# A two-layer transformer block with expert rows: token tiles in turn, and x with a token on each partition from layer 0's rows on

## The chip, the cores and the metric

The kernel runs on one core of a Trainium2 chip. The core has five engines that follow their own instruction streams in order: TensorE (PE in the profile, its weight loads PEld), VectorE (DVE), ScalarE (ACT), GpSimd (POOL) and SyncE (SP). Data come from memory through the core's 16 DMA engines, asked for by queues that belong to SP, ACT and POOL. The metric is the device time of one execution in microseconds.

## The reference

256 tokens of width 1024 pass two layers. Layer 0 mixes tokens by window attention and a gated MLP, layer 1 by means over windows. Each layer then has an expert stage ("PEER"): every token scores 128 + 128 sub-keys for each of 8 heads, takes the best 16 pairs, and gathers 16 rows of `down` and `up` for each head. Cut to what matters here:

```python
def multiscale_pool(h, w_pool, scale):        # layer 1's mixer
    ...                                       # cs: running sums of h, in 4 groups of 256 columns
    for g, w in enumerate((2, 4, 8, 16)):
        lo, hi = jnp.clip(t - w // 2, 0, L_), jnp.clip(t + w // 2, 0, L_)
        mean = (cs[:, hi, g] - cs[:, lo, g]) / (hi - lo)
        diffs.append(mean - hf[:, :, g])
    pooled = jnp.stack(diffs, axis=2)
    return jnp.einsum('blgc,gce->blge', pooled, w_pool).reshape(B_, L_, D_MODEL) * scale

def peer_ffn(h, w_q, sub_keys, down, up):
    q = (xb @ w_q).reshape(n, 8, 2, 128)
    s = jnp.einsum('thpk,pnk->thpn', q, sub_keys)
    s_top, i_top = lax.top_k(s, 16)
    ...                                       # 256 sums of pairs, best 16 again -> idx, gate (softmax)
    act = jax.nn.gelu(jnp.einsum('thkd,td->thk', down[idx], xb))
    return jnp.einsum('thk,thkd->td', gate * act, up[idx])

for l in range(2):
    m = jax.nn.silu(c) @ mod_w[l] + mod_b[l]  # -> sh1, sc1, g1, sh2, sc2, g2
    h = rms_norm(x, norm1_g[l]) * (1 + sc1) + sh1
    y = attn_gmlp_mixer(h, ...) if l == 0 else multiscale_pool(h, pool_w, pool_scale)
    x = x + g1 * y
    h2 = rms_norm(x, norm2_g[l]) * (1 + sc2) + sh2
    x = x + g2 * peer_ffn(h2, ...)
return rms_norm(x, final_g)
```

All arithmetic that decides the choice of rows is held at single precision: a product of two matrices is made from three, with each operand split into a high and a low part (`sH`, `sL` for weights, `xH`, `xL` for x).

## The kernel before

**Layers and stages.** `attention_gmlp` computes layer 0's mixer. Then `peer_rows(0)`, `pool_mixer`, `peer_rows(1)` and `final` follow. From `peer_rows` on, the instructions of each engine run in the order in which the code issues them. x is held as `xT`, a channel on each partition, in 8 blocks of 128 channels by 256 tokens.

**The projection in `peer_rows`.** `norm_split` (L299 to L308) makes xH and xL, `pair_mm` (L340 to L343) the first head's queries, `tile_mm` (L317 to L319) those of the other heads, two tiles a head. The weights come through `Stream`: SP loads an item of 512 KB (three buffers), ScalarE casts half of it to `sH` (L105), VectorE subtracts to `sL` (L108). `scores` (L1040, L1043) follows one tile behind. `advance` puts four steps of `choose` on VectorE behind each tile from head 1 on. `choose` is the selection for one unit (a token tile and a head) in some 22 steps: MAX8, FIND_INDEX8 and MATCH_REPLACE8 (L954 to L962), comparisons (L992 to L997), the row numbers `eid` (L998), and ScalarE's Exp for the gate (L1001). `rows_of` (L950, L951) turns h2 to a token on each partition. Units go head by head, both token tiles of a head in turn.

**The rows.** A ring of 12 slots of 1 MB holds what comes from memory for 128 tokens at a time: one row number k of a unit, `down` and `up` side by side. `fetch` asks for the next row (L1018, on POOL) as soon as the next slot of the ring is free. During the projection xH, xL and hq take three slots. When it is over, the loop over 256 rows (16 units of 16) begins: a dot of `down` with h2 on VectorE (L1102), with two steps of `choose` behind each; behind every fourth row a Gelu on ScalarE (L1108); one row later `weigh` makes the four weights (L1089) and `add_up` makes for each row a diagonal on ScalarE (`dgr`, L1076), two matmuls of `up` into PSUM (L1079) and gives the slot back. In layer 0, VectorE also computes 56 products of modulation weights in this loop, one at every fourth row (L884).

**Between the layers.** When all rows have been asked for, `after_rows` takes ring slots for pool weights and prepares them, a step for every row added up. `residual` copies the four sums out of PSUM (L908, L909), turns them back (L914) and adds them to xT (L916); sums of squares go over partitions by matmul (L175). `pool_mixer` multiplies by pool_w first (L1226), then takes the means (L1254). Layer 1 ends in `residual` and `final`, which turns x back by a matmul with the final gains (L1270) and writes four pieces (L1290).

## Time and profile before

| | |
|---|---|
| median of 3 runs | 1755.05 us (1752.7 to 1755.4) |
| the profiled execution | 1751.43 us |
| its span, first to last instruction | 1749.4 us |
| busy: PE, DVE, POOL, ACT | 1352.9, 1197.8, 741.6, 466.0 us |
| moved by DMA | 622.52 MB, mean 356 GB/s |
| mean granted TensorE clock | 0.896 of full |

Engines are busy for part of the span only, and the DMA share, in tenths for 40 slices of the span, is 9 (90% or more) in all but a few slices. In a timeline, a row is an instruction or a run of equal ones: start, duration, engine, line, operation, what it writes and reads, and in brackets how long the engine was idle before it and what ended that.

### The profile page before, as it was taken

Reading aid. Unit: us, or ns where it says so; the run is one execution under the profiler, and the core shown is the slowest. Engines: PE = TensorE matmul, PEld = TensorE weight load, DVE = VectorE, ACT = ScalarE, POOL = GpSimd, SP = SyncE. Lnnn points to the kernel's source line nnn. Section 1 sums busy time; section 2 is a strip of 40 time slices with the busy share of each in tenths; the row PEclk is TensorE's granted clock in tenths of the full one; section 3 lists DMA queues with packets and bytes.
Section 4 is the critical chain, followed back from the end, with each engine's and each line's share of the span. In section 5 each row is a group of like instructions: output and inputs, shape, how many; then the busy total and the mean of one; then the engine's idle time right before and its main releaser. Section 6 shows DMA issues by size and latency. Waiting matters only on the chain. (4 is left out here: it accounts for less than half of the span.)

```text
span 1749.4 us, 15727 instructions
## 1 busy us (share of the span) xinstructions
PE 1352.9 (77%) x4148; PEld 691.8 (40%) x4148; DVE 1197.8 (68%) x2910; ACT 466.0 (27%) x1176; POOL 741.6 (42%) x632
## 2 busy tenths in 40 slices
PE   7988897677767677767777797877877887777776
PEld 3865793233223233223233387333333333333333
DVE  6987768877787776555554377877777775545443
ACT  3555553222222121111111353222222222111112
POOL 3535433443444434444444133544444454544442
PEclk8987998988888978988888899899998898999899
DMA  7434578999999999999999328799999999999993
GB/s 291 164 109 158 170 280 323 419 419 419 418 419 418 419 418 418 419 419 419 419 419 414 135 86 342 321 419 420 419 419 420 419 420 420 420 420 420 418 420 124
DMA packets 97867, 622.52 MB, mean 356 GB/s; under 512 B 11250, under 2 KB 11762, under 8 KB 31860
## 3 DMA queue, kind: packets, MB, share of 16 engines
q0 software_dynamic: 73728, 536.90, 74.3%
q1 hardware_dynamic: 23328, 83.82, 12.9%
q8 instruction: 34, 0.56, 0.1%
q10 hardware_dynamic: 724, 0.80, 0.1%
q14 instruction: 53, 0.43, 0.1%
HBM read 620.44 MB, written 1.05 MB: 355 GB/s over the span
## 5 line engine op out<-in xcount | busy, mean ns | idle before, releaser
L1079 PE MATMUL ps_big<-row,dgr 128*128 128x512 f32 x2048 | 1033.4, 664 | 340.3 <-ACT dgr L1076 340.3
L1018 POOL DMA_INDIRECT row<-in_DU,eid x512 | 609.6, 1191 | 801.7 <-PE ps_big L1079 537.1
L1102 DVE SCALAR_TENSOR_TENSOR row<-row,h 128x1024 f32<-128x1024 f32 x512 | 627.2, 1225 | 419.4 <-DMA row<-in_DU,eid 407.8
L1079 PEld LDWEIGHTS ps_big<-row,dgr 128*128 128x128 f32 x2048 | 424.2, 212 | 948.1 <-issue 504.8
L1076 ACT ACTIVATE dgr<-cf,cr 128x128 f32<-128x128 f32 x512 | 164.0, 390 | 276.9 <-DVE cr L1089 275.2
L1108 ACT ACTIVATE actr<-actr 128x4 f32<-128x4 f32 x128 | 26.3, 205 | 701.0 <-DVE row L1102 700.8
L108 DVE TENSOR_TENSOR sL<-raw,sH 128x512 fp32r<-128x512 f32 x75 | 57.8, 798 | 30.7 <-ACT sH L105 24.9
L884 DVE SCALAR_TENSOR_TENSOR md<-md,crowb 128x1024 f32<-128x1024 f32 x56 | 68.1, 1216 | 0.0
L317 PE MATMUL ps_a<-row,sH 128*128 128x256 f32 x224 | 65.3, 291 | 2.3 <-ACT sH L105 1.4
L318 PE MATMUL ps_a<-row,sH 128*128 128x256 f32 x224 | 63.1, 282 | 1.0 <-issue 1.0
L319 PE MATMUL ps_a<-row,sL 128*128 128x256 f32 x224 | 63.5, 283 | 0.5 <-DVE sL L108 0.4
L105 ACT CAST sH<-raw 128x512 fp32r<-128x512 f32 x84 | 49.2, 619 | 24.5 <-DMA raw<-in_w_q 10.9
L511 PE MATMUL ps_big<-sH,hH 128*128 128x256 f32 x128 | 38.4, 306 | 8.6 <-ACT sH L105 6.1
L317 PEld LDWEIGHTS ps_a<-row,sH 128*128 128x128 f32 x224 | 42.8, 191 | 4.1 <-ACT qTp L1051 2.1
L319 PEld LDWEIGHTS ps_a<-row,sL 128*128 128x128 f32 x224 | 42.7, 191 | 1.7 <-DVE sL L108 1.1
L318 PEld LDWEIGHTS ps_a<-row,sH 128*128 128x128 f32 x224 | 42.8, 191 | 0.7 <-issue 0.7
L1102 DVE DVE_READ_ACCUMULATOR row<-row,h 128x1 f32 x512 | 42.2, 82 | 0.0
L512 PE MATMUL ps_big<-sL,hH 128*128 128x256 f32 x128 | 38.2, 301 | 2.6 <-DVE sL L108 2.5
L1001 ACT ACTIVATE gater<-best,z 128x16 f32<-128x16 f32 x32 | 9.8, 308 | 106.8 <-DVE z L1000 106.7
L513 PE MATMUL ps_big<-sH,hL 128*128 128x256 f32 x128 | 37.2, 296 | 0.1
L1001 ACT ACT_TABLE_LOAD x28 | 35.9, 1283 | 0.5
L1108 ACT ACT_TABLE_LOAD x28 | 35.9, 1283 | 0.4
(265 smaller groups left out, 1315.6 us busy)
## 6 DMA issues: line engine op xcount, KB each, us to landing
md<-in_modT SPq DMA_DIRECT2D x56, 512.0 KB, 7.9
raw<-in_w_q SPq DMA_DIRECT2D x32, 512.0 KB, 3.3
raw<-in_modT SPq DMA_DIRECT2D x19, 512.0 KB, 4.7
row<-in_DU,eid POOLq DMA_INDIRECT x512, 18.5
pro<-in_modT SPq DMA_DIRECT2D x11, 512.0 KB, 3.7
pro<-in_modA SPq DMA_DIRECT2D x8, 512.0 KB, 6.7
raw<-in_in_w SPq DMA_DIRECT2D x8, 512.0 KB, 4.4
pro<-in_in_w SPq DMA_DIRECT2D x6, 512.0 KB
```

What stands on the lines that cost most here:

```text
L105: k.nc.scalar.copy(hi, src)
L108: eng.tensor_sub(lo, src, hi)
L317: nc.tensor.matmul(ps, lhsT=hi[:, i], rhs=xh[:, kb], start=(first and i == 0), stop=False)
L318: nc.tensor.matmul(ps, lhsT=hi[:, i], rhs=xl[:, kb], start=False, stop=False)
L319: nc.tensor.matmul(ps, lhsT=lo[:, i], rhs=xh[:, kb], start=False, stop=(last and i == 3))
L884: self.nc.vector.scalar_tensor_tensor(raw, raw, 1.0, crow, op0=OP.mult, op1=OP.mult, accum_out=self.m[:, l, j:j + 1])
L1001: nc.scalar.activation(g, best, AF.Exp, bias=z[:, 0:1], scale=1.0, accum_out=z[:, 1:2])
L1018: nc.gpsimd.indirect_dma_start(r, None, a[f"DU{l}"], bass.IndirectOffsetOnAxis(ap=eid[:, tt, h, k:k + 1], axis=0))
L1076: nc.scalar.activation(dg, self.ident, AF.Copy, scale=cw[:, tt, s:s + 1])
L1079: nc.tensor.matmul(acc[2 * tt + hf], lhsT=dg, rhs=r[:, D + 512 * hf:D + 512 * hf + 512], start=(s == 0), stop=(s == P - 1))
L1102: nc.vector.scalar_tensor_tensor(r[:, :D], r[:, :D], 1.0, h2[:, tt], op0=OP.mult, op1=OP.mult, accum_out=act[:, tt, s:s + 1])
L1108: nc.scalar.activation(act[:, tt, s], act[:, tt, s], AF.Gelu_apprx_tanh)
```

## The change

What is done otherwise, in the order of the program:

- `norm_in` now makes xH, xL and h2 for layer 0. x itself is turned to a token on each partition (`self.x`) beside the first rows, and stays so.
- Units go token tile by token tile: eight heads of tile 0, then eight of tile 1. In layer 0, `scores` of head 0 follow `pair_mm` at once and up to 30 steps of `choose` behind them; in layer 1 head 0 is projected for tile 0 alone, scored and chosen, before tile 1.
- The ring has 10 slots instead of 12. Modulation products use the weights' three buffers, at every row with k % 3 == 2.
- Small steps go beside the rows (`beside`, one a row): turning x, spreading a vector of 1024 over partitions (`rowvec`: eight transposes, two copies), and, when token tile 0's rows are added up, its `tile_end`: x plus gate times sum, square with sum, inverse root.
- `after_rows` runs two steps for every row added up. It loads pool_w and the means' matrix, spreads five vectors, and makes tile 0's h1.
- `pool_mixer` takes the means first and multiplies by pool_w then; each token tile gets product, sum, inverse, scaling and shift on VectorE, then transposes to xH and xL.
- The last unit's batches are 4, 4, 4, 2, 1, 1. `residual` and `final` are gone: tile 1's `tile_end` scales and writes two pieces, tile 0's were written in the middle of layer 1.

```diff
-RING = 12
+RING = 10
...
-        units = [(tt, h) for h in range(8) for tt in range(2)]
+        units = [(tt, h) for tt in range(2) for h in range(8)]
...
+        prev = []
+        if l == 0:
+            first = self.pair_mm(xH, xL)
+        else:
+            halves = [st.next() for _ in range(4)]
+            first = [self.bank("a") for _ in range(2)]
+            qT = tk.tile([P, 2, T], F32, name="qTp", bufs=2)
+            for tt in range(2):
+                ts = slice(tt * P, (tt + 1) * P)
+                for p in range(2):
+                    for hf in range(2):
+                        hi, lo = halves[2 * p + hf]
+                        self.half_mm(first[p][:, ts], 4 * hf, hf == 0, hf == 1, hi, lo, xH[:, :, ts], xL[:, :, ts])
+                    nc.scalar.copy(qT[:, p, ts], first[p][:, ts])
+                scores(0, qT, (tt,))
+                if tt == 0:
+                    advance(30)
+            st.ahead(LOOK)
...
+            if h == 0:
+                scores(h, qT)
+                advance(30)
...
+            ends = (4, 8, 12, 14, 15, 16) if n == len(units) - 1 else (4, 8, 12, 16)
...
+    def add_rows(self, tt, src, row, ss):
...
+        for hf in range(2):
...
+            nc.vector.tensor_mul(t, src[hf], row[:, hs])
+            yield
+            nc.vector.tensor_add(self.x[:, tt, hs], self.x[:, tt, hs], t)
...
+            nc.scalar.activation(sq, self.x[:, tt, hs], AF.Square, scale=1.0 / 32, accum_out=ss[:, hf:hf + 1])
+            yield
...
+        for k, col in enumerate(vecs):
+            if k % 2 == 0:
+                t = yield from self.carve(2, D)
+            self.rows_.append(t[:, k % 2])
+            yield from self.rowvec(t[:, k % 2], col)
+        self.h1 = yield from self.carve(2, D)
+        yield from self.scaled(0, self.y[0], *self.rows_[:2], self.h1)
...
+        for tt in range(2):
...
+            run(self.add_rows(tt, z[tt], gs, ss))
+            y = self.inverse(ss, True)
+            run(self.scaled(tt, y, G2, sh2, h2))
+            for hf in range(2):
...
+                for i in range(4):
...
+                    nc.tensor.transpose(pt[:, i * P:(i + 1) * P], h2[:, tt, kb * P:(kb + 1) * P], self.ident)
...
+                nc.scalar.copy(xH[o], p3)
+                nc.vector.tensor_sub(xL[o], p3, xH[o])
```

What this does to the engines' streams, at three places. First ScalarE in layer 0, behind `pair_mm`: casts of weights (`sH`), copies of queries (`qTp`), of scores (`sc`) and of h2, and the Exp of a unit (`gater`). Before:

```order
L1051 COPY qTp<-ps_a 128x256 [waits PE_49] x2
L105 CAST sH<-raw 128x512
L105 CAST sH<-raw 128x512 [waits DMAHW6_49,Activation_49]
L1051 COPY qTp<-ps_a 128x256 [waits PE_49]
L1043 COPY sc<-ps_w 128x512 [waits PE_49]
L951 COPY h_2002<-ps_a 128x512 [waits PE_49]
L105 CAST sH<-raw 128x512 [waits DVE_49]
```

and now:

```order
L1115 COPY qTp<-ps_a 128x256 [waits PE_49] x2
L1090 COPY sc<-ps_w 128x256 [waits PE_49] x2
L1046 ACT_TABLE_LOAD
L1046 ACTIVATE gater,z<-best,z 128x16 [waits DVE_49]
L105 CAST sH<-raw 128x512
L105 CAST sH<-raw 128x512 [waits DMAHW7_49,Pool_49]
L1115 COPY qTp<-ps_a 128x256 [waits PE_49]
L923 COPY h_2004<-ps_a 128x512 [waits PE_49]
```

The scores' copies and the first unit's Exp have moved ahead of the casts for head 1 and of its first copy; the Exp stood some 20 rows further down.

Second ScalarE near the end of layer 0's rows: the diagonals (`dgr`) of a batch of four rows and what stands between them. Before:

```order
L1076 ACTIVATE dgr<-cf,cr 128x128 [waits DVE_49,PE_49]
L1076 ACTIVATE dgr<-cf,cr 128x128 [waits PE_49,Activation_49] x3
L1108 ACTIVATE actr<-actr 128x4 [waits DVE_49]
L1076 ACTIVATE dgr<-cf,cr 128x128 [waits DVE_49,PE_49]
L1076 ACTIVATE dgr<-cf,cr 128x128 [waits PE_49,Activation_49] x2
L1188 CAST ones_r<-ones 128x128
L1213 ACTIVATE row<-row,g_5463 128x256 [waits DMASW6_49,DMASW2_49,DMAHW6_49,DVE_49,PE_49]
L1213 ACTIVATE row<-row,g_5463 128x256
L1076 ACTIVATE dgr<-cf,cr 128x128 [waits Activation_49]
```

and now, where a `row` is a ring slot that takes the spread vectors:

```order
L1142 ACTIVATE dgr<-cf,cr 128x128 [waits DVE_49,PE_49]
L938 COPY row<-ps_a 128x512 [waits DMASW2_49,DMASW4_49,DMASW0_49,DMASW6_49,PE_49,Pool_49]
L938 COPY row<-ps_a 128x512 [waits PE_49]
L1142 ACTIVATE dgr<-cf,cr 128x128 [waits Activation_49]
L938 COPY row<-ps_a 128x512 [waits PE_49] x2
L1142 ACTIVATE dgr<-cf,cr 128x128 [waits Activation_49]
L938 COPY row<-ps_a 128x512 [waits DMASW5_49,DMASW3_49,DMASW7_49,DMASW1_49,PE_49]
L938 COPY row<-ps_a 128x512 [waits PE_49]
L1142 ACTIVATE dgr<-cf,cr 128x128 [waits Activation_49]
L938 COPY row<-ps_a 128x512 [waits PE_49] x2
```

Behind each diagonal there now stand two copies of a spread vector's halves, which wait for TensorE's transposes.

Third VectorE in layer 0, where token tile 0's last rows are weighed: `row,actr` is a dot, `cr` the weights of a batch, `eq` to `gater` steps of `choose`. Before, at the same count of dots:

```order
L1102 SCALAR_TENSOR_TENSOR row,actr<-row,h_2002 128x1024 [waits DMASW0_49,PE_49]
L1089 TENSOR_TENSOR cr<-actr,gater 128x4 [waits Activation_49]
L962 MAX_INDEX ix<-v,wkt 128x8 [waits DVE_49]
L954 MAX v<-sc 128x8
L1102 SCALAR_TENSOR_TENSOR row,actr<-row,h_2002 128x1024 [waits DMASW1_49,PE_49]
L956 MAX_INDEX ix<-v,sc 128x8 [waits DVE_49]
L958 MATCH_REPLACE wkt<-v,sc 128x128
```

and now:

```order
L1177 SCALAR_TENSOR_TENSOR row,actr<-row,h_2004 128x1024 [waits DMASW0_49,PE_49]
L1158 TENSOR_TENSOR cr<-actr,gater 128x4 [waits Activation_49]
L1040 TENSOR_TENSOR eq<-eq,ixf 128x512 [waits DVE_49]
L1042 TENSOR_REDUCE e_4438<-eq 128x32 [waits DVE_49]
L1043 SCALAR_TENSOR_TENSOR eid<-e_4438 128x16 [waits DVE_49]
L1045 TENSOR_SCALAR z<-best 128x1
L951 TENSOR_TENSOR tx<-ps_big,rg 128x512 [waits PE_49]
L1177 SCALAR_TENSOR_TENSOR row,actr<-row,h_2004 128x1024 [waits DMASW1_49]
L1048 RECIPROCAL z<-z 128x1 [waits Activation_49]
```

The product of the sum in PSUM (`ps_big`) with the spread gate now stands between the weights and the next dot.

## Rows read from the trace of the kernel before

**Rows 1.** The page: busy DMA and GB/s in 40 equal slices; the queue of gathers.
```profile
DMA  7434578999999999999999328799999999999993
GB/s 291 164 109 158 170 280 323 419 419 419 418 419 418 419 418 418 419 419 419 419 419 414 135 86 342 321 419 420 419 419 420 419 420 420 420 420 420 418 420 124
q0 software_dynamic: 73728, 536.90, 74.3%
```
**Rows 2.** Timeline, steady rows of layer 1: start, duration in us, engine, line.
```profile
1695.80 1.22 DVE L1102 SCALAR_TENSOR_TENSOR row<-row,h 128x1024 f32<-128x1024 f32 x1 [1.26 <-DMA row<-in_DU,eid]
1697.66 7.13 PE L1079 MATMUL ps_big<-row,dgr 128*128 128x512 f32 x16 [2.55 <-ACT dgr L1076]
1698.30 1.22 DVE L1102 SCALAR_TENSOR_TENSOR row<-row,h 128x1024 f32<-128x1024 f32 x1 [1.19 <-DMA row<-in_DU,eid]
```
**Rows 3.** Windows of 10 us: PE, PEld, DVE, ACT, POOL, PEclk, DMA share, GB/s.
```profile
280.00:290.00 10.00, 8.69 (x15) 3.88 (x16) 9.20 (x31) 3.38 (x11) 2.74 (x3) 0.69 0.27 88
980.00:990.00 10.00, 7.84 (x15) 3.13 (x14) 4.80 (x11) 3.42 (x8) 1.35 (x1) 0.84 0.03 11
1090.00:1100.00 10.00, 1.63 (x2) 0.83 (x3) 8.93 (x26) 3.17 (x8) 0.70 (x1) 0.59 0.51 199
```
**Rows 4.** Timeline, start of layer 0's rows.
```profile
223.23 0.37 ACT L1051 COPY qTp<-ps_a 128x256 f32<-128x256 f32 x1 [1.05 <-PE ps_a L319]
236.78 1.17 POOL L1018 DMA_INDIRECT row<-in_DU,eid  x1 [14.27 <-DVE z L1000]
269.69 1.21 DVE L1102 SCALAR_TENSOR_TENSOR row<-row,h 128x1024 f32<-128x1024 f32 x1
285.37 1.20 POOL L1018 DMA_INDIRECT row<-in_DU,eid  x1 [13.66 <-PE ps_big L1079]
```
**Rows 5.** Timeline of VectorE, the first unit's choice in layer 0.
```profile
220.68 0.30 DVE L954 MAX8 v<-sc 128x8 f32<-128x128 f32 x1 [1.55 <-ACT sc L1043]
229.31 1.29 DVE L108 TENSOR_TENSOR sL<-raw,sH 128x512 fp32r<-128x512 f32 x2 [1.59 <-ACT sH L105]
236.31 0.18 DVE L998 SCALAR_TENSOR_TENSOR eid<-e 128x16 uint32<-128x16 f32 x1
```
**Rows 6.** Gathers from issue to landing: window 1130 to 1400, then the whole run.
```profile
DMA to landing us min/median/max: 15.0/17.8/19.2
DMA to landing us min/median/max: 7.7/18.5/22.7
```
**Rows 7.** Groups by shape: busy us, mean ns of one, idle before, its releaser.
```profile
L951 ACT COPY h<-ps_a 128x512 f32<-128x512 f32 x8 | 4.7, 591 | 0.3
L909 DVE COPY row<-ps_big 128x512 f32<-128x512 f32 x4 | 2.8, 689 | 11.8 <-PE ps_big L1079 11.8
L1226 PE MATMUL ps_big<-row,xT 128*128 128x256 f32 x32 | 7.5, 382 | 0.0
```
**Rows 8.** The chain that ended last: start, us, four transposes in a row.
```profile
1035.25 0.44 PE ps_a L950 x4
```
**Rows 9.** Timeline, from layer 0's last rows to layer 1's first dot.
```profile
976.66 0.16 DVE L1089 TENSOR_TENSOR cr<-actr,gater 128x4 f32<-128x4 f32 x1
985.28 1.23 DVE L1102 SCALAR_TENSOR_TENSOR row<-row,h 128x1024 f32<-128x1024 f32 x1 [1.26 <-DMA row<-in_DU,eid]
989.19 8.83 PE L1079 MATMUL ps_big<-row,dgr 128*128 128x512 f32 x16 [2.16 <-ACT dgr L1076]
1031.27 0.39 PE L317 MATMUL ps_a<-row,sH 128*128 128x256 f32 x1 [0.34 <-ACT qTp L1051]
1052.56 1.04 POOL L1018 DMA_INDIRECT row<-in_DU,eid  x1 [14.85 <-PE ps_a L319]
1086.74 1.21 DVE L1102 SCALAR_TENSOR_TENSOR row<-row,h 128x1024 f32<-128x1024 f32 x1
```
**Rows 10.** Timeline, the tail: the last dot and the last write.
```profile
1723.22 1.23 DVE L1102 SCALAR_TENSOR_TENSOR row<-row,h 128x1024 f32<-128x1024 f32 x1 [1.26 <-DMA row<-in_DU,eid]
1745.02 0.35 ACTq L1290 DMA_DIRECT2D out<-row  x1
```

## What the change will do to the time: the prediction

> **What bounds the kernel now.** I read the page's slices first: from about 290 us to 975 and again from 1110 to 1715 the transfers run at 418 to 420 GB/s, and the queue of gathers alone carries 537 MB [rows 1]. In those stretches a row of experts (1 MB for 128 tokens) lands every 2.49 us, which the distance of two dots shows, and VectorE waits about 1.2 us for each [rows 2]. So a stretch of rows can only be shortened by starting its stream earlier or by moving fewer bytes. The bytes stay the same. What is left are the places where the stream stands still, read from windows and timelines: the start of layer 0's rows (share 0.27 from 280 to 290), the passage between the layers (0.03 in 980 to 990, 0.51 in 1090 to 1100 [rows 3]) and the tail.
>
> How a stream starts: the first gathers go out during the projection, but only into free slots of the ring. Dots begin when the projection is over. The first slot of the loop comes back 15.7 us after the first dot (269.69 to the gather at 285.37 [rows 4]), and until then nothing can be asked for. Hence the start of the steady stream is set by the first dot plus about 21 us, and by how many rows were in before it: 12 now. It is not set by the first gather.
>
> **The change part by part.** I sum against the profiled execution, 1751.4 us; its span is 1749.4, and the median of the runs shown is 3.6 above it.
>
> *Layer 0, first unit at once.* Token tile 0's head 0 is now chosen in one piece. In the trace that choice takes 15.8 us from the first MAX8 to the written indices, with four pairs of splits between (1.3 us a pair) and a wait of 1.6 [rows 5]: 9 us alone. It starts near 217.9, 2.8 before the first MAX8 of now, since three splits instead of five and no tile of TensorE stand ahead of it, so the first gather is ready near 227 instead of 236.8. But ScalarE has the unit's Exp ahead of the next casts and of the copy of head 1's first half out of its bank. With both banks taken, TensorE's next half starts near 229.1, and its copy, which stands at 223.23 now [rows 4], comes at 232.1: 8.9 us late. The rest up to the first dot took 46.5 us (223.23 to 269.69). I keep that; if waiting for weights behind gathers absorbed some, it would be less by up to 5. First dot 278.6, **+8.9** (4 to 11).
>
> *Ring of 10.* Ten rows are in before the loop's first release, where 12 were. Two rows at 2.49 are fetched later, **+5.0** in each layer. That is the same arithmetic in layer 1, where xH and xL leave eight slots and then two.
>
> *Ring of 10 in the steady stretch.* With 12 slots a row lands 15.0 to 19.2 us after its issue in layer 1, and the shortest landing in the whole run took 7.7 [rows 6]. Two slots fewer take 5.0 off: 10.0 at the least, still 2.3 over 7.7. So nothing by itself; from both sides, 0 to 0.3 us for each of the 128 batches if 10.0 is too little, which is a rival below.
>
> *Layer's middle.* The tile end of token tile 0 puts its product with PSUM on VectorE right behind one dot. It waits for the four rows whose weights were made just before: 7.13 us of TensorE [rows 2], about 6 us behind the next batch's due time. Of that 10.0 - 7.7 = 2.3 and some slack in slots hide half; **+2.5** a layer, 0 to 5. The Trainium skill, DMA: Bandwidth & Descriptors, section on the anatomy of a gpsimd DMA, gives a fixed 2.0 us plus bytes over 436 GB/s, an estimate of 4.4 us for a row. By it the slack would be 5.6 us and the two waits would cost nothing, the sum 5 lower. I go by the 7.7 of the trace.
>
> *End of layer 0's rows.* The ten half vectors of pool gains and shifts are now spread over rows by transposes, eight behind each of the rows 248 to 252, and each group's two copies stand on ScalarE ahead of the next row's diagonal. A row then costs a chain: its own passes 1.78 (7.13 over four [rows 2]), two copies of 0.59 [rows 7], twice four transposes of 0.44 together [rows 8], and the diagonal, about 4.0 us with overlap. Rows 248 to 251 start after the batch weights at 976.66 [rows 9], the first at half clock as now. So 977.4, 983.6, 987.6, 991.6; then the Gelu of rows 252 and 253, their weights, row 252 at 996.1, row 253 at 1000.0, rows 254 and 255 behind it. VectorE adds to it: h1 of tile 0 needs the slot of row 251 and stands ahead of the last dot. The sums are done near 1005.4; now 989.19 + 8.83 = 998.0 [rows 9]. The smaller last batches save work here (one row behind the table load instead of four), but it is behind this chain. **+7.4** (0 to 12); if the copies cost ScalarE nothing, the small batches would win some 5.
>
> *Pool stage.* From there VectorE holds one chain. I count 32 operations of 512 columns (0.65 to 0.69 each, as the copy out of PSUM [rows 7]), 21 us; four copies of 256, 1.4; three inverses of about 2.3 (square with sum, Sqrt, five columns), 7; and 4.5 of waits for means, pool products (16 matmuls, 7.5 us [rows 7]) and transposes. That is 34 us until the second tile's xL. Head 0 for the first tile starts behind the second tile's transposes, since TensorE's order has them first: 48 matmuls of 128 columns, 3 to 5 us, then copy, scores, copy 1.5 and the choice 9. First gather 48.5 us after the sums, at 1054; now 1052.56 [rows 9]. The second tile's queries wait on ScalarE behind the Exp, and head 1's casts behind them: head 1 starts 51.5 us after the sums, at 1056.9, where it starts at 1031.27 now.
>
> *Rest of the projection.* Now 1031.27 to the first dot at 1086.74, 55.5 us with its wait for weights behind nine gathers. Less the 1.8 us of four groups of transposes (0.44 [rows 8]) that layer 1 no longer needs: 53.6. First dot at 1110.5 on the clock of before, **+23.8** in all, the 7.4 included (bounds 13 and 33: the chain, the count of operations, and whether early gathers slow the weights less).
>
> After such a pause TensorE restarts at half clock in the trace (granted 0.59 in 1090 to 1100 after 2 us of work in 10 [rows 3]). The Trainium skill, TensorE: Matmul & The Clock Gate, Part 1, says the gate is closed by default and activity opens it; by it head 1 would lose some 2 us after its 8 us pause, and the sum would be 2 higher. I leave it in the bounds.
>
> *Tail.* Now 1724.5 (end of the last dot at 1723.22) to 1749.4, 24.9 us. After: the Gelu, table load and one diagonal 2.9, one row 1.8, then no transposes but product and sum for each half 2.6, square 0.8, inverse 1.5, last scaling 1.3, and 4.4 from the last issue at 1745.02 to the end [rows 10], with overlap 14.6. **-10.3** (-12 to -8).
>
> Sum: 8.9 + 5.0 + 2.5 + 23.8 + 5.0 + 2.5 - 10.3 = +37.4. On the profiled 1751.4 that is 1788.8, on the median of 1755.05 it is 1792.4. I forecast **1790**. Vectors of layer 0's middle, mods at every third row and the two rowvecs of layer 1 I cost at nothing: VectorE waits 1.2 us a row for DMA [rows 2], and each adds under that to a row; with choice and mods together a row has little left, and if that cover were gone each of some 45 mods could cost 0.3 us, 13 in all.
>
> **The rivals.**
> A (other side): *the stream counts from the first gather.* If rows asked for earlier move the whole stream, because the projection's pause is swallowed by weights it would have waited for anyway, layer 0 gains the 9.8 us from 236.8 to 227, layer 1 is even (1054 against 1052.6) and the tail gives 10: 1755 - 20 = 1735. It decides if the first dots come no later than 269.7 and 100 us after layer 0's last dot. For it: weights do wait behind gathers. Against it: at 280 to 290 the DMA stands at 0.27 with every slot full [rows 3], so earlier rows only wait longer. 0.09.
> B: *ten slots are too few.* If 10.0 us from issue to landing leaves the DMA dry by 0.3 us a batch, 128 batches cost 38 us on top: 1828. For it: the middle of a layer eats the slack. Against it: the 7.7. 0.09.
> C: *the spreading is hidden and the pool stage is quicker than counted,* so that the gains of a row per partition (no sums over partitions, no norm split) show: the passage costs +6 instead of +23.8, the rest of the sum stays, 1772. 0.12.
> D: *the change doesn't do what it says:* the early unit's Exp isn't reached early, the order of before remains, and only ring and tail act: +5 +5 -10, 1755. 0.03.
>
> **How the numbers follow.** Forecast 0.67, A 0.09, B 0.09, C 0.12, D 0.03. Low end: 4 + 5 + 0 + 13 + 5 + 0 - 12 = +15 on 1755, 1770, which takes in C; high end: 11 + 5 + 5 + 33 + 5 + 5 - 8 = +56, 1811, which I cut to 1809. Left out are A, B and D, and the forecast's edges. Faster by over 0.2% (3.5 us, about what a measurement tells from no change): A and a little of the rest, 0.10; the same: D and an edge, 0.05; slower 0.85.
>
> **What would show it.** In the new profile: first gather of layer 0 near 227 but first dot near 278; DMA share under 0.3 for some 15 us before the first release in both layers; the four transposes between the passes of rows 248 to 252 and the sums about 19 us after the last row lands; layer 1's first gather some 65 us after that row's dot was due and first dot some 124; landing times near 12.5 us; the tail near 15. Wrong: dots that start as early as before (A), a share under 0.97 in the long stretches (B), head 1 of layer 1 less than 40 us after the sums (C).

## The result, and the profile after

The changed kernel takes 1793.56 us (median of 4 runs, 1791.34 to 1796.62) beside 1753.88 for the kernel before: a ratio of 1.0232, 95% interval 1.0205 to 1.0259, or 39.7 us more. A second set, beside its own runs of the kernel before, gave 1793.04 and a ratio of 1.0237. The forecast was 1790.

First the page of the changed kernel: span, busy DMA share in tenths and GB/s in 40 slices of 44.9 us. Compare [rows 1].

```profile
span 1794.8 us, 15679 instructions
DMA  7434476999999989999999207599999989999995
GB/s 290 159 123 153 147 307 257 420 420 420 419 418 414 412 332 409 420 420 420 421 418 421 110 0 309 195 421 421 415 422 413 418 359 416 422 421 421 422 421 247
```

The long stretches run at the same 412 to 422 GB/s as before. What is new are two dips where there were none (332 GB/s in slice 15 and 359 in slice 33, each in the middle of a layer) and a deeper, longer hole between the layers (110, 0, 309, 195 against 135, 86, 342 before). A program's dots come one after the other, 512 in all, so the time of the n-th dot in either trace tells where the difference arises. After less before, from the two traces of the changed kernel:

| | first trace | second trace | forecast, added up |
|---|---|---|---|
| row 0 of layer 0 | +10.3 | +10.0 | +8.9 |
| row 16 | +11.1 | +10.8 | +13.9 |
| row 254 of layer 0 | +14.6 | +11.1 | +16.4 |
| row 0 of layer 1 | +48.5 | +45.3 | +40.2 |
| row 32 of layer 1 | +49.8 | +46.3 | +45.2 |
| row 255 of layer 1 | +55.1 | +51.6 | +47.7 |
| end of the span | +45.4 | +41.9 | +37.4 |

So the passage between the layers costs 34 us, not 23.8; the starts of the two layers 12 in all, not 18.9; the rest is near the forecast. Now the places, in timelines (start, duration, engine, line; in brackets the idle time before and what ended it). Layer 0's start: first gather, first dot, first slot back. Compare [rows 4].

```profile
226.98 1.16 POOL L1062 DMA_INDIRECT row<-in_DU,eid  x1 [5.84 <-DVE z L1045]
279.96 1.21 DVE L1177 SCALAR_TENSOR_TENSOR row<-row,h 128x1024 f32<-128x1024 f32 x1
292.45 0.95 POOL L1062 DMA_INDIRECT row<-in_DU,eid  x1 [8.87 <-DVE ij L1034]
```

The rows are asked for 9.8 us sooner and the first dot is 10.3 us later, as forecast. But the first slot comes back 12.5 us after the first dot, and not 15.7. Before, the first Gelu stood on ScalarE behind the Exp of a unit, which waited for its choice on VectorE between the dots:

```profile
278.72 0.31 ACT L1001 ACTIVATE gater<-best,z 128x16 f32<-128x16 f32 x1 [8.16 <-DVE z L1000]
```

With the first unit chosen ahead no Exp stands before that Gelu, and the steps of a choice between the first four dots are shorter ones: the fourth dot begins 5.0 us after the first, where it was 6.2.

The middle of layer 0, where the tile end of token tile 0 begins, then windows there and in layer 1 (busy PE, PEld, DVE, ACT, POOL, granted clock, DMA share, GB/s):

```profile
644.88 10.14 PE L1145 MATMUL ps_big<-row,dgr 128*128 128x512 f32 x16 [6.04 <-ACT dgr L1142]
654.21 0.69 DVE L951 TENSOR_TENSOR tx<-ps_big,rg 128x512 f32<-128x512 f32 x1 [8.27 <-PE ps_big L1145]
663.60 1.28 ACT L1184 ACT_TABLE_LOAD   x1
665.14 0.16 DVE L1158 TENSOR_TENSOR cr<-actr,gater 128x4 f32<-128x4 f32 x1 [1.21 <-ACT actr L1184]
665.85 9.90 PE L1145 MATMUL ps_big<-row,dgr 128*128 128x512 f32 x16 [10.82 <-ACT dgr L1142]
```

```profile
645.00:650.00 5.00, 5.00 (x6) 2.08 (x7) 0.90 (x3) 2.39 (x6) 0.94 (x1) 0.50 1.01 418
650.00:660.00 10.00, 5.03 (x11) 1.86 (x9) 5.72 (x14) 0.72 (x2) 3.42 (x3) 0.84 0.94 337
660.00:670.00 10.00, 4.15 (x5) 1.85 (x6) 8.51 (x26) 3.49 (x8) 0.10 (x1) 0.50 0.40 167
1470.00:1480.00 10.00, 7.21 (x12) 3.18 (x13) 8.51 (x30) 3.30 (x8) 2.11 (x2) 0.65 0.52 190
```

VectorE waits 8.27 us for the four rows' passes, which take 10.14 us here instead of 7.13, after 6.04 us in which TensorE did nothing and partly at the lower clock (a granted 0.50 from 645 to 650, which is 1.2 GHz; 1.00 is 2.4). Behind that wait stand the next dots, behind those their Gelu (with a table load), and the next four rows' passes begin 21 us after the last four did. Meanwhile no slot comes back, and the DMA share falls to 0.40.

The end of layer 0's rows, with the vectors spread between the passes (L936 transposes, L938 copies):

```profile
996.95 1.98 PE L1145 MATMUL ps_big<-row,dgr 128*128 128x512 f32 x4 [0.97 <-ACT dgr L1142]
998.77 1.04 PE L936 MATMUL ps_a<-cf,m 128*128 128x128 f32 x8
999.41 1.07 ACT L938 COPY row<-ps_a 128x512 f32<-128x512 f32 x2 [2.51 <-PE ps_a L936]
1000.83 1.98 PE L1145 MATMUL ps_big<-row,dgr 128*128 128x512 f32 x4 [1.02 <-ACT dgr L1142]
1008.38 0.16 DVE L1158 TENSOR_TENSOR cr<-actr,gater 128x2 f32<-128x2 f32 x1 [9.77 <-ACT actr L1184]
1012.92 5.42 PE L1145 MATMUL ps_big<-row,dgr 128*128 128x512 f32 x12 [1.03 <-ACT dgr L1142]
1017.51 0.69 DVE L951 TENSOR_TENSOR tx<-ps_big,rg 128x512 f32<-128x512 f32 x1 [2.90 <-PE ps_big L1145]
```

Each row takes 3.88 us (996.95 to 1000.83) through passes, transposes, copies and diagonal; the Gelu of the next two rows stands behind the copies, and VectorE waits 9.77 us for it. The forecast had 4.0 a row and the same order. The sums are done when the last passes end, at 1018.3.

The passage: ScalarE's Exp of layer 1's first unit, first gather, a cast that waits for its weights, first dot, first slot back; then windows of 5 us. Compare [rows 9].

```profile
1074.72 0.31 ACT L1046 ACTIVATE gater<-best,z 128x16 f32<-128x16 f32 x1 [9.17 <-DVE z L1045]
1075.38 0.94 POOL L1062 DMA_INDIRECT row<-in_DU,eid  x1 [90.55 <-DVE z L1048]
1088.75 0.62 ACT L105 CAST sH<-raw 128x512 fp32r<-128x512 f32 x1 [5.42 <-DMA raw<-in_w_q]
1135.23 1.21 DVE L1177 SCALAR_TENSOR_TENSOR row<-row,h 128x1024 f32<-128x1024 f32 x1
1148.08 1.31 POOL L1062 DMA_INDIRECT row<-in_DU,eid  x1 [9.23 <-DVE ijf L1035]
```

```profile
1055.00:1060.00 5.00, 5.00 (x26) 5.00 (x25) 0.20 (x1) 1.25 (x3) 0.00 (x0) 0.50 0.00 0
1070.00:1075.00 5.00, 5.00 (x25) 5.00 (x24) 4.41 (x14) 0.28 (x2) 0.00 (x0) 0.50 0.00 0
1085.00:1090.00 5.00, 3.59 (x30) 3.39 (x29) 0.60 (x1) 1.25 (x3) 0.23 (x1) 1.00 1.01 412
1090.00:1095.00 5.00, 1.46 (x8) 1.28 (x7) 2.57 (x9) 1.35 (x5) 0.00 (x0) 0.63 1.01 420
```

Three things are to be seen. TensorE is busy all the time from 1055 to 1075 at a granted clock of 0.50, with head 0's products of 128 columns, 25 in 5 us. ScalarE waits 9.17 us for the choice, with the copies and casts that the next head needs behind it. And from 1085 to 1095, with head 1 under way, the DMA is full with the eight rows asked for early, while TensorE does 5 of 10 us, waiting for weights that come behind them.

The tail, last dot and last write, compare [rows 10]: 16.4 us from the dot's start to the end of the span against 26.1, the gain that was forecast.

```profile
1778.36 1.23 DVE L1177 SCALAR_TENSOR_TENSOR row<-row,h 128x1024 f32<-128x1024 f32 x1 [2.12 <-DMA row<-in_DU,eid]
1791.42 0.35 ACTq L1217 DMA_DIRECT2D out<-tx  x1
```

### The profile page after: what moved, and what is told of

Its sections match the earlier page's. It is cut to its first block, busy times and chain, and to the rows that moved or that the text cites. A ratio compares the mean times of both kernels' runs of the same rounds, so it can differ in the third digit from the quotient of the medians.

```text
span 1794.8 us, 15679 instructions
## 1 busy us (share of the span) xinstructions
PE 1366.8 (76%) x4144; PEld 707.0 (39%) x4144; DVE 1208.9 (67%) x2935; ACT 468.3 (26%) x1196; POOL 723.0 (40%) x596
## 4 chain that ended last, share of the span: by engine, by line
DMA 32%; issue 20%; DVE 17%; POOL 15%; PE 14%; ACT 3%; POOLq 0%; DVEq 0%; ACTq 0%
DMA row<-in_DU,eid 30%; POOL row L1062 14%; DVE row L1177 5%; PE ps_big L1145 3%; PE ps_a L317 1%; PE ps_a L319 1%; PE ps_a L318 1%; DMA raw<-in_w_q 1%; PE ps_w L1087 1%; DVE raw L884 1%; DVE sL L108 1%; PE ps_big L805 1%; PE ps_big L388 1%; PE ps_w L796 1%; DVE dscr L396 0%
## 5 line engine op out<-in xcount | busy, mean ns | idle before, releaser
L1062 POOL DMA_INDIRECT row<-in_DU,eid x512 | 622.1, 1215 | 923.8 <-PE ps_big L1145 607.6
L1184 ACT ACTIVATE actr<-actr 128x4 f32<-128x4 f32 (+1 forms) x132 | 27.1, 205 | 654.3 <-DVE row L1177 654.1
L317 PE MATMUL ps_a<-row,sH 128*128 128x256 f32 (+1 forms) x256 | 80.6, 315 | 8.7 <-ACT qTp L1115 7.7
L319 PE MATMUL ps_a<-row,sL 128*128 128x256 f32 (+1 forms) x256 | 78.8, 308 | 0.0
L108 DVE TENSOR_TENSOR sL<-raw,sH 128x512 fp32r<-128x512 f32 x74 | 52.9, 745 | 38.3 <-ACT sH L105 35.4
L318 PE MATMUL ps_a<-row,sH 128*128 128x256 f32 (+1 forms) x256 | 78.7, 307 | 0.0
L884 DVE SCALAR_TENSOR_TENSOR raw<-raw,crowb 128x1024 f32<-128x1024 f32 x61 | 75.4, 1237 | 0.0
L317 PEld LDWEIGHTS ps_a<-row,sH 128*128 128x128 f32 x256 | 55.6, 217 | 9.5 <-ACT qTp L1115 8.2
L318 PEld LDWEIGHTS ps_a<-row,sH 128*128 128x128 f32 x256 | 55.5, 217 | 0.0
L319 PEld LDWEIGHTS ps_a<-row,sL 128*128 128x128 f32 x256 | 55.4, 216 | 0.2 <-DVE sL L108 0.2
L1158 DVE TENSOR_TENSOR cr<-actr,gater 128x4 f32<-128x4 f32 (+1 forms) x132 | 20.9, 158 | 24.0 <-ACT actr L1184 24.0
## 6 DMA issues: line engine op xcount, KB each, us to landing
row<-in_DU,eid POOLq DMA_INDIRECT x512, 10.7
```

The source lines that it names most:

```text
L108: eng.tensor_sub(lo, src, hi)
L317: nc.tensor.matmul(ps, lhsT=hi[:, i], rhs=xh[:, kb], start=(first and i == 0), stop=False)
L318: nc.tensor.matmul(ps, lhsT=hi[:, i], rhs=xl[:, kb], start=False, stop=False)
L319: nc.tensor.matmul(ps, lhsT=lo[:, i], rhs=xh[:, kb], start=False, stop=(last and i == 3))
L884: self.nc.vector.scalar_tensor_tensor(raw, raw, 1.0, crow, op0=OP.mult, op1=OP.mult, accum_out=self.m[:, l, j:j + 1])
L1062: nc.gpsimd.indirect_dma_start(r, None, a[f"DU{l}"], bass.IndirectOffsetOnAxis(ap=eid[:, tt, h, k:k + 1], axis=0))
```

## Experiments

Each kernel ran beside the kernel before on the same chip. The numbers below are medians less the median of before in the same set, so the changed kernel stands at +39.7 and +41.5. The 95% intervals of the ratios reach 2 to 5 us to either side, so two kernels that differ by under some 4 us are not told apart by their times alone.

**The changed kernel again**, for the second column above.

> The changed kernel once more, unaltered, beside the others of this set, so that they are compared on the same chip, and a second trace shows how far the places differ from one execution to the next. Every theory: a ratio to the kernel before of 1.023, and the first dots and the first gathers within 1 to 3 us of the first trace.

+41.5, ratio 1.0237 (1.0219 to 1.0254). The first gather of layer 1 is at 1072.1 and its first dot at 1132.1, both some 3.2 before the first trace; that much (3.5) is there at row 254 already.

**No early unit in layer 0.**

```diff
-            if h == 0:
-                scores(h, qT)
-                advance(30)
-            else:
-                prev.append((h, qT))
+            prev.append((h, qT))
```

> The changed kernel with one part undone: in layer 0 the scores of head 0 go one tile behind again and no unit is chosen before head 1. Theory (a stream's start is set by the first dot, and the early Exp and choice hold TensorE up): first gather back from 227 to about 237, but first dot from 280.0 to about 271, and the whole run 9 us shorter, about 1784.5. Rival A (the stream counts from the first gather): first gather 10 later and the run 10 longer, about 1803. Second rival (the projection would have waited for weights behind the gathers anyway): first dot stays within 2 us of 280, 1793.6.

+40.3: about 1 us from the changed kernel, on either side, so the 9 of the theory and the 10 of rival A are both out. The timeline shows why: first gather, first dot, first slot back.

```profile
238.26 1.16 POOL L1062 DMA_INDIRECT row<-in_DU,eid  x1 [16.04 <-DVE z L1045]
271.63 1.21 DVE L1173 SCALAR_TENSOR_TENSOR row<-row,h 128x1024 f32<-128x1024 f32 x1
287.77 1.20 POOL L1062 DMA_INDIRECT row<-in_DU,eid  x1 [10.20 <-PE ps_big L1141]
```

The first dot is 8.3 us earlier, as forecast, but the first slot comes back 16.1 us after it and not 12.5, so only 4.7 are left there; row 248 is 3.3 to 5.7 earlier. The first gather, 11 us later, does no harm. In the trace the rows follow neither the first gather nor the first dot, but the first release; that the run's time gains these 3 to 6 us is not shown.

**Tile end 12 rows later.**

```diff
-            if tt == 0 and s == P - 1:
+            if tt == 1 and s == 11:
                 self.bg.append(self.tile_end(l, 0, acc[:2], False))
```

> The changed kernel with the tile end of token tile 0 begun 12 rows later in both layers, so that VectorE finds the four sums finished and does not wait 8.3 us for TensorE behind one dot. Theory (the two dips in the DMA share, some 8 and 7 us by the dots' times, are that wait and what queues behind it): both dips go, 1793.6 - 15 = about 1778.5. The prediction's size of the term (2.5 a layer): 1788.5. Rival (what the middle loses is made good later, since only the start and the end of a stretch count): 1793.6.

+33.2, so 6.5 to 8.3 less; ratio 1.0196 (1.0172 to 1.0220). The same windows show no dip:

```profile
660.00:670.00 10.00, 4.41 (x9) 1.65 (x8) 8.27 (x23) 2.56 (x6) 2.26 (x3) 0.74 1.01 423
1470.00:1480.00 10.00, 5.09 (x9) 1.98 (x8) 7.98 (x17) 3.89 (x10) 2.15 (x3) 0.86 1.01 423
```

The wait is the cause of the dips. But a part of each is made good: rows 384 to 392 of all take 27.4 us with the wait and 19.9 without, rows 392 to 448 then 138.8 and 142.5. Net, the middle costs 4 to 6 us in layer 0 (rows 112 to 240: 360.5 and 362.5 against 356.3) and 3.5 in layer 1. The truth lies between the theory (15) and the prediction's 5.

**Vectors spread one row ahead.** Transposes of vector k behind one row's passes, its copies behind the next row's diagonal, one step a row:

```diff
+        for k in range(6):
+            if k:
+                ...
+                for hf in range(2):
+                    nc.scalar.copy(t[:, (k - 1) % 2, hf * 512:(hf + 1) * 512], ps[hf])
+            if k < 5:
+                ps = [self.bank("a") for _ in range(2)]
+                for i in range(8):
+                    nc.tensor.transpose(ps[i // 4][:, i % 4 * P:(i % 4 + 1) * P],
+                                        vecs[k][:, i:i + 1].to_broadcast([P, P]), self.ident)
+            yield
...
                     next(after, None)
-                    next(after, None)
```

> The changed kernel with the five spread vectors of layer 0's last rows in another order: the transposes of a vector stand behind one row's passes and its two copies behind the next row's diagonal, one vector a row, so that a copy no longer waits for the row's passes. Theory (the chain passes - transposes - copies - diagonal, 3.9 us a row, holds up the last rows): a row 3.0 us, the Gelu of rows 252 and 253 no longer behind ten copies, sums 5 to 7 us earlier and the run with them, about 1787.5. Rival (the last row's landing or VectorE's h1 sets the end of the rows, and the chain is hidden): 1793.6.

+37.3, so 2 to 4 less, which the intervals do not tell from nothing. A row takes 2.6 us instead of 3.88 (TensorE's timeline, passes and transposes):

```profile
992.71 1.88 PE L1145 MATMUL ps_big<-row,dgr 128*128 128x512 f32 x4
994.42 1.04 PE L1254 MATMUL ps_a<-cf,m 128*128 128x128 f32 x8
995.30 1.88 PE L1145 MATMUL ps_big<-row,dgr 128*128 128x512 f32 x4
```

The first product of tile 1's end comes at 1007.85 where it was at 1014.3 and 1017.5 in the two traces of the changed kernel, and layer 1's first dot is 6.7 and 9.9 earlier. The runs show less than the traces do. The chain of copies is real and was sized about right, 3.88 us a row for 4.0; what it costs the whole run is not settled.

**TensorE kept busy in the pool stage.**

```diff
+            if tt == 0:
+                ps = self.bank("a")
+                for _ in range(36):
+                    nc.tensor.matmul(ps[:, :P], lhsT=self.ones, rhs=self.ones, start=True, stop=True)
```

> The changed kernel with 36 products of ones (128x128, unread) put on TensorE between the two token tiles' transposes of the pool stage, where it idles 7.8 us; they write a bank that nobody reads. Theory (the idle time leaves TensorE at the granted 0.50 for the 27 us from 1050 on, in which it is busy throughout with head 0 of layer 1): granted clock near 1 there, 48 products of a token tile in about 5.2 us instead of 10.4, first gather of layer 1 some 5 earlier, head 1 and first dot up to 10 earlier, 1784 to 1788. Rival 1 (the clock falls all the same): granted 0.5, 1793.6. Rival 2 (the clock comes back but the first dot stays, because the weights behind the gathers or ScalarE's casts set it): first gather 5 earlier, first dot within 2 us, 1793.6.

+34.9, so 5 to 7 less, just beyond the intervals. Windows, where head 0 of layer 1 now runs:

```profile
1050.00:1055.00 5.00, 5.00 (x47) 5.00 (x46) 1.29 (x2) 2.83 (x5) 0.00 (x0) 1.00 0.00 0
```

Products of 128 columns now start 0.11 us apart instead of 0.21, and token tile 0's 48 take 5.5 us instead of 10.5. From the last dot to layer 1's first gather it is 60.1 us instead of 65.5, and from that gather to the first dot 60.0 as before: the 5 us of token tile 0's products are won, the rest of the projection stays. The second tile's 48 products are 5 us quicker too, but that wins nothing: TensorE then waits 4.88 us for the copy behind the Exp, and the Exp waits 9.18 us for the choice as before.

**A pair and no early unit in layer 1; a pair with the early unit.** Both project head 0 for both token tiles at once; the first one also chooses no unit before head 1.

```diff
-        if l == 0:
+        if True:
             first = self.pair_mm(xH, xL)
...
-        for h in range(0 if l == 0 else 1, 8):
+        for h in range(8):
...
-            if h == 0:
+            if h == 0 and l == 0:
```

(the last two lines only in the kernel without the early unit).

> The changed kernel with one part undone in layer 1 alone: head 0 is projected for both token tiles as a pair, its scores go one tile behind, and no unit is chosen before head 1. Theory (the first dot of a layer, not its first gather, sets its stream; early gathers hold weights up): first gather of layer 1 about 15 to 20 later than 1075, first dot 1 to 6 earlier than 1135, the run 1 to 6 shorter than the changed kernel. Rival A (the stream counts from the first gather): 15 longer. Rival 2 (the per-tile projection was right: its weights and its choice lie beside each other): 0 to 3 longer.

> The changed kernel with head 0 of layer 1 projected for both token tiles as a pair, but, unlike the run before with a pair, its unit of token tile 0 still chosen at once. It splits what that run won (17 us; first dot 25 earlier) between the products by token tile and the early unit. Theory (a product of 128 columns takes 0.213 us at the lower clock, as one of 256 does, so the token tiles double 48 products, and the clock stays down with them; the early unit's Exp in layer 1 costs what it does in layer 0, 8 at the first dot): first dot of layer 1 about 17 earlier than in the changed kernel, near 1115 to 1118, the run 9 to 13 shorter, about 1781. Rival 1 (the early unit is all of it): 0 to 3 shorter, 1791. Rival 2 (the token tiles are all of it): 17 shorter, 1776.

Without the early unit +24.3, 15 to 17 less, far more than either theory gave; with it +30.3, 9 to 11 less. Timeline of the first, first gather and first dot, and a window:

```profile
1079.39 0.94 POOL L1062 DMA_INDIRECT row<-in_DU,eid  x1 [95.06 <-PE ps_a L319]
1109.64 1.21 DVE L1177 SCALAR_TENSOR_TENSOR row<-row,h 128x1024 f32<-128x1024 f32 x1
```

```profile
1055.00:1060.00 5.00, 4.66 (x39) 4.45 (x39) 1.96 (x4) 2.83 (x6) 0.00 (x0) 1.00 0.30 105
```

The first dot is 22 to 26 us earlier, though the first gather is 4 to 7 later. The kernel with the early unit asks for its rows at 1068.7, 10.7 sooner than this one, has its first dot at 1120.8, 11.1 later, and takes 6 us longer. So the products by token tile cost some 10 us, their lower clock included, and the early unit in layer 1 another 6. The reason for the first is seen in two pieces of TensorE's timeline, at a granted 0.50, of the changed kernel and then of the one with the pair:

```profile
1054.18 0.41 PE L317 MATMUL ps_a<-row,sH 128*128 128x128 f32 x1
1054.40 0.41 PE L318 MATMUL ps_a<-row,sH 128*128 128x128 f32 x1
```

```profile
1051.53 0.41 PE L340 MATMUL ps_a<-row,sH 128*128 128x256 f32 x1
1051.74 0.41 PE L341 MATMUL ps_a<-row,sL 128*128 128x256 f32 x1
```

Products of 128 and of 256 columns both start every 0.21 us. At the full clock those of 128 columns start 0.11 us apart and those of 256 0.12. Cut in halves, head 0 costs TensorE almost twice; and with the clock that stays down besides, its products take 21.6 us in the changed kernel against 7.3 with the pair. The Trainium skill, TensorE: Matmul & The Clock Gate, section on the back-to-back issue gap, says that in a stream of weight loads and matmuls the spacing is set by both; the windows agree, with PEld busy 5.00 of 5.00 us.

**The kernel before with ten slots.** `RING = 12` to `RING = 10`, nothing else.

> The kernel before with 10 ring slots instead of 12 and nothing else. Theory of the prediction (two rows fewer in before a layer's first release, 2.49 us each, nothing in the steady stretch): +5.0 a layer, 10 in all, ratio 1.0057. What the dots of the changed kernel suggest (2.5 to 3 us between first dot and row 16 of layer 1, and the release comes 3 us sooner after the first dot): +3 a layer, 6 in all, ratio 1.0034. Rival B (ten slots too few in the steady stretch, 0.3 us a batch): +38, ratio 1.022.

+9.1, ratio 1.0053 (1.0034 to 1.0072): near the 5.0 a layer of the prediction, with 3 a layer at the interval's end. Row 32 to row 248 of layer 1 take 545.9 us against 544.5, so the steady stretch needs no more than ten. The gathers of the changed kernel, which has ten too, from issue to landing (least, median, longest), compare [rows 6]; this trace times 64 of the 512, as that one does:

```profile
DMA to landing us min/median/max: 5.6/10.7/14.9
```

Two traces that time all 512 compare better: a median of 12.4 us in this kernel, and 17.4 in the one with twelve slots and small last batches further down, 5.0 apart, which is two rows at 2.49. The least is 5.5 and 5.6.

**Four parts undone at once:** no early unit in either layer, a pair, the later tile end, the vectors ahead.

> The changed kernel with four edits at once: no early unit in either layer and a pair in layer 1, the tile end 12 rows later, the vectors spread one row ahead. What stays of the change: units token tile by token tile, x with a token a partition, means ahead of pool_w, ten ring slots, small last batches. Theory (the four prices are separate places and add): 1793.0 - 17.3 - 9.8 - 5.8 - 2.7 = 1757.4, ratio 1.0035, with row 0 of layer 1 about 36 after the kernel before's less these, near 1089. Rival 1 (they overlap, since the later places have slack once the earlier are mended): 1765 to 1770. Rival 2 (the rest of the change is worth a gain once these are gone): 1745.

+6.0, ratio 1.0032 (1.0018 to 1.0045), as expected. By the differences above the single prices add to 24 to 31 us, and together the edits take out 34 to 36, so they do not overlap. What is left of the change: row 16 of layer 0 stands 6.7 later than before, layer 1's first dot 10.9, its row 32 15.5, and the tail gives 9 back. Row 254 to layer 1's first dot is 110.9 us, 7 more than before.

**The kernel before with small last batches, with small batches at both ends, and with a bare start.**

```diff
+            ends = {0: (1, 2, 4, 8, 12, 16), 15: (4, 8, 12, 14, 15, 16)}.get(n, (4, 8, 12, 16))
+            for k0, k1 in zip((0,) + ends, ends):
...
-                    advance(2, 8)
+                    advance(0 if n == 0 and k < 8 else 2, 8)
```

The first kernel has the entry for unit 15 alone, the second both, the third the last line too.

> The kernel before with the last unit's batches of 4, 4, 4, 2, 1, 1 rows in both layers and nothing else. Theory (behind the last dot stand the weights, diagonals and passes of up to five rows, of which small batches leave one or two): 2 to 4 us shorter at the end of each layer, 5 to 8 in all, ratio 0.996. Rival 1 (small batches bring more Gelus between the diagonals on ScalarE and win nothing): 1.000. Rival 2 (the tail's gain in the changed kernel came from dropping the transposes alone): within 1 us, 1.000.

> The kernel before with small batches at both ends of a layer's rows: the first unit 1, 1, 2, 4, 4, 4 and the last 4, 4, 4, 2, 1, 1. Theory (a stream's start is the first release, 15.7 us after the first dot, behind a batch of four; the DMA idles 8 to 10 us for it): the first slot back some 8 us sooner, the hole in the DMA share half as long, 3 to 5 a layer on top of the 8.7 of small last batches: 1751.5 - 8.7 - 8 = about 1735, ratio 0.990. Rival (VectorE is the bound there, 9.2 to 9.8 of 10 us busy with dots and choices, and the later rows are no sooner): as with small last batches alone, 1743, ratio 0.996.

> The kernel before with small batches at both ends, as the run before, and without the two steps of a choice behind each of a layer's first eight rows (the choices of these rows' units are finished by then; the later ones move 16 steps back). Theory (from the first dot to the steady stretch VectorE sets the pace, 9.8 of 10 us busy, a row 2.2 us of which a dot is 1.23; the DMA idles meanwhile): rows 0 to 8 in 11 us instead of 16.6, slots back 4 to 5 sooner, 2 to 4 a layer: ratio 0.988 to 0.990 against 0.9928 with the steps. Rival (the choices put off are missed later: units 3 and 4 are late and the gathers wait for their row numbers): 0.993 to 0.997. Second rival (TensorE, at the lower clock there, sets the releases): 0.9928.

-8.7 (ratio 0.9958, 0.9943 to 0.9973), -11.7 (0.9928, 0.9907 to 0.9950) and -22.8 (0.9876, 0.9854 to 0.9897), 1730.93 us: faster than both kernels.

The second's lead on the first, 3 us, is within the intervals; the third's on the second is not. The first did not win where it was expected to. At layer 0's end the copy of the sums comes at 990.80 instead of 997.19, of which 1.8 were there at the last dot, and layer 1's first dot is 9.9 sooner. But the tail takes 27.0 us from the last dot against 26.1: the sums are copied 2.2 sooner after it, and then the column sums and the products with the final gains run at the lower clock (a granted 0.50 from 1728 on, 1.00 in the same place before):

```profile
1727.07 1.92 PE L1271 MATMUL ps_big<-row,xT 128*128 128x128 f32 x8
1728.78 3.41 PE L175 MATMUL ps_w<-ones,row 128*128 128x1 f32 x16
```

1.06 and 1.84 us in the kernel before. The other two show what the start of a stream hangs on. First dot and first slot back, of the second kernel, then of the third:

```profile
268.74 1.21 DVE L1103 SCALAR_TENSOR_TENSOR row<-row,h 128x1024 f32<-128x1024 f32 x1
276.50 1.19 POOL L1018 DMA_INDIRECT row<-in_DU,eid  x1 [5.75 <-DVE row L1103]
```

```profile
267.30 1.21 DVE L1103 SCALAR_TENSOR_TENSOR row<-row,h 128x1024 f32<-128x1024 f32 x1
274.11 1.26 POOL L1018 DMA_INDIRECT row<-in_DU,eid  x1 [4.80 <-PE ps_big L1079]
```

7.8 and 6.8 us instead of 15.7 [rows 4]. But after its early first slots the second kernel is held by VectorE, 9.86 of 10 us busy with dots and choices:

```profile
280.00:290.00 10.00, 6.59 (x13) 2.81 (x14) 9.86 (x33) 2.18 (x7) 2.60 (x3) 0.91 0.91 341
```

Rows 0 to 8 take 16.6 us there as before, and 9.5 in the third, whose windows over the old hole read

```profile
270.00:280.00 10.00, 9.66 (x19) 4.36 (x20) 10.00 (x24) 3.75 (x12) 4.78 (x4) 0.83 1.00 397
280.00:290.00 10.00, 7.30 (x18) 3.01 (x17) 8.93 (x27) 3.87 (x9) 6.59 (x5) 1.00 0.99 403
```

where the DMA share from 280 to 290 was 0.27 [rows 3].

## Why the prediction was right, and where its terms were not

**The time.** 1793.6 against 1790, and slower as forecast. Two errors of size offset each other: the passage cost 10 us more than its term and the two starts 7 less. That the number came so near is in part luck.

**Layer 0, first unit at once (+8.9).** The mechanism and its two dates were right: first gather 226.98 for 227, first dot 279.96 for 278.6. The price was not: undoing it moves row 248 by 3 to 6 and the run by about 1. The step that failed is the sentence that the steady stretch starts at the first dot plus about 21 us; it kept the 15.7 from first dot to first release, which is 12.5 where no Exp of a unit stands ahead of the first Gelu. Layer 1's start cost 1 instead of 5 in the same way (first dot 1135.23 to first slot back 1148.08, 12.9).

**Ring of 10 (+5.0 a layer, nothing in the steady stretch).** Right: +9.1 for both layers in the kernel before. Landings fell by 5.0 in the median, 17.4 to 12.4. The 7.7 that the prediction took for the least was the least of the 64 landings that its trace times; with twelve slots too the least of all 512 is 5.6. The conclusion stands, with more slack than counted. The estimate of 4.4 from the Trainium skill's DMA: Bandwidth & Descriptors (anatomy of a gpsimd DMA) was not reached: the least landing in any trace is 5.4.

**Layer's middle (+2.5 a layer).** Mechanism right, size too small: 4 to 6 and 3.5. The prediction counted four rows' passes at 7.13; they took 10.14 at the lower clock, and behind the wait stood the next batch's Gelu with a table load and its weights, 21 us between two batches. The slack of slots hid about half of the dip, as it had said, but of a larger one. What the prediction drew from the Trainium skill's DMA: Bandwidth & Descriptors (anatomy of a gpsimd DMA), that the two waits would cost nothing, does not hold here.

**End of layer 0's rows (+7.4).** Sums at 1018.3 (1012.92 + 5.42), 20.3 after those of before, of which row 254 brings 14.6: 5.7. Spreading ahead, which keeps the work and breaks the chain, wins 6.5 and 9.7 at that place against the two traces, 2 to 4 in the runs.

**Pool stage and passage (+23.8 in all).** This is the term that was mis-sized: 34, beyond its bound of 33. VectorE's chain of 34 us took 37 (1018.3 to 1055.2), so the count of its operations was good. The step that failed is the next: "48 matmuls of 128 columns, 3 to 5 us". They took 10.5, because TensorE stayed at 0.50; the prediction had priced the lower clock at 2 us, for head 1 and not for these, and kept that in the bounds. At the full clock they took 5.5. Head 1 began 59 us after the sums instead of 51.5, and the rest of the projection took 57.7 instead of 53.6, with 5.42 and 2.34 us of waits for weights behind the early rows. The runs give 5 to 7 back for the clock alone, 9 to 11 for the pair, and 6 more for the early unit; the pair brings the clock back too, so the first two do not add.

**Tail (-10.3).** Right: -9.7 in both traces.

**The rivals.** A, the stream counts from the first gather, is refuted twice: rows asked for 11 us later cost nothing in layer 0, and 10.7 later won 6 in layer 1. B, ten slots too few, is refuted by the ring of 10. C, a passage of +6, is what the four edits together leave (7), and not what the change does. D did not happen.

**Layer 0 between rows 16 and 254.** The changed kernel loses nothing net there in its second trace, though the middle costs 4 to 6 there. From row 16's dot to row 248's it moves 273.1 to 273.3 MB by the traces, where the kernel before moved 275.9, two rows and one modulation weight more; at 418 GB/s the difference is some 6 us, which makes it up. In between it is up to 32 us behind (row 192), since its modulation weights come sooner: 13.0 MB against 10.5 from row 112 to 192, and 0.6 against 7.3 from there to 248.

**Left open.** That the runs show less of the spreading than the traces is not settled. Products that keep the clock up in the tail of the kernel with small last batches were not tried.

## What to carry to other kernels

A ring that is full waits for its first release: shorten what stands between the first row and its slot (a small first batch, no other work on the engine that uses the rows), and not the time to the first request. A result that is wanted early must not be waited for on an in-order engine that others need for the next stage. Before a product is cut into column blocks to start sooner, look whether its spacing is set by columns at all; and an idle time just ahead of a chain of products can be paid for in their clock.

## What the runs showed of the hardware

- From 1055 to 1075 TensorE ran products of 128 columns back to back, and its granted clock stayed at 0.50 (1.2 GHz) all that time, as it did in that place in four more traces. With products of 256 columns in the same place it was back at 1.00 (2.4 GHz) some 3 us after the pair's start, in three traces; with 36 products of ones ahead of them, those of 128 ran at 1.00.
- Products of 128 and 256 columns of this type start equally far apart at the lower clock (0.21 us) and nearly so at the full one (0.11 and 0.12).
- With ten slots a row of 1 MB lands in a median of 12.4 us instead of 17.4 with twelve, at 416 and 420 GB/s in the steady stretch: the longer landings were queueing.
